# Row products that read PSUM, GpSimd low parts and later activation loads in a one-core transformer block

## The chip, the core and the metric

The kernel runs on one core of a Trainium2 chip. The core has a matrix engine (TensorE, PE in the profile), a vector engine (VectorE, DVE), a scalar engine (ScalarE, ACT), GpSimd (POOL) and a sync engine (SyncE, SP) that here only issues DMAs. ACT and POOL issue DMAs as well. Each engine works through its own queue in order. The engines share the on-chip memory SBUF; matmuls write into eight banks of a second memory, PSUM, each 128 partitions by 512 float32.

The metric is the time of one execution on the device in microseconds. A kernel's time is the median of several executions, and beside it stands one execution recorded by the profiler.

## What is computed

The reference is one block of a streaming encoder over 512 frames and 16 meta tokens of width 2048: two attention branches, gated and merged, and then a product-key expert layer with 16,384 experts of which each token uses 128. The expert layer matters here:

```python
def block(xb):
    q = (xb @ w_q).reshape(PEER_BLOCK, PEER_HEADS, 2, PEER_HALF)
    s = jnp.einsum('thcd,hcnd->thcn', q, sub_keys).astype(jnp.float32)
    s1, i1 = lax.top_k(s[:, :, 0], PEER_TOPK)
    s2, i2 = lax.top_k(s[:, :, 1], PEER_TOPK)
...
    h = jnp.einsum('tkd,td->tk', u[idx], xb)
    act = (g * jax.nn.gelu(h.astype(jnp.float32), approximate=False)).astype(xb.dtype)
    return jnp.einsum('tk,tkd->td', act, v[idx])
```

Then the result is added to the residual, and a final RMSNorm over the 2048 features ends the kernel.

## The kernel before

**Splitting of operands.** All large products are done as three passes on a high and a low part of each operand (`mm3`, L259). `wtile` (L233) loads a raw weight tile of 128x1024 (SP, L244), makes the high part on ACT (L246) and the low part by a subtraction (L247), on DVE unless an engine is named. It notes the last ACT instruction in `more["last"]`, and the last low part in `more["lo"]` if it was not on POOL.

**The stages in time.** Attention and gates run to about 1310 us. Then comes the score stage: 16 blocks `hc`, each with two weight tiles `wq` and a query result `ps`, which ACT and DVE split into `pqh` and `pql` (L265, L266), and 12 small matmuls of the block before (`scores`, L1138), which DVE ranks with `top16` (L940). Most low parts of this stage are made on POOL.

After it the expert layer has two phases. In the first, 128 blocks `e` compute h for 128 experts each, for the first 324 tokens (ND): `u_products` (L1115) has two halves `hf`, each one weight tile and 24 matmuls; ACT takes the Gelu of the result (L1407) and sends it to DRAM. In the second, 32 steps `i` of eight weight tiles multiply the gated activations with v and add into `acc` (L1541). The activations of a group of four blocks come back from DRAM with two loads, `hin` (L1363) and `gin` (L1355); they are gated (`gated`, L1369) and split (`group_split`, L1442).

**The remaining 188 tokens** go another way, by gathered rows. `send` (L1063) has POOL issue an indirect DMA that brings one row of u or v for each of 128 partitions; `row_step` (L1087) has DVE multiply it. A u row is multiplied with the tokens' activations and summed over the row (L1095); the activations of the first 128 tokens (part 0) are `xg`, 128x2048, in SBUF. `PACE` (L1051) ties the number of rows done to the block: 20 before the first block, 38 by block 14, 108 by block 60. By block 16 that is some 41 rows, all of part 0.

**Routing.** `route` (L967) finds the experts of the first 324 tokens in small DVE steps between the blocks (`beside`, L1391); `gates_of` (L1263) turns them into a dense gate.

**Order.** The framework places each instruction of a queue when its inputs are ready by its own model, in the order of the program among those that are ready; a dependency without synchronisation (`NOSYNC`) only keeps one instruction behind another in that order. So a load can be placed long before the line that asks for it is reached, and then its queue waits at it until its buffer is free. `spread_rows` (L957), called at block 64, issues eight small loads on SP.

**PSUM.** One pool of eight banks serves all stages (`ps_tile`, L225).

**The end.** Each finished chunk of `acc` is squared on ACT into `fsq` (one buffer) and added to `ssf` on DVE (`fin_add`, L1453). `fin_out` (L1460) sums `ssf` over partitions with a matmul by ones, forms the reciprocal root (`rstd`, L298), scales 16 chunks on DVE (L1465) and stores them from SP (L1467).

## Time and profile before

| | us |
|---|---|
| median of 3 runs | 3480.44 |
| lowest and highest | 3478.97, 3483.09 |
| the profiled execution | 3478.44 |
| its span | 3476.4 |

The span runs from the first to the last instruction of the program. A row of a view names a line of the kernel, an engine, an operation and the tiles as out<-in. Behind a bar, or in square brackets, stands the idle time of the engine before the instruction and what ended it: "<-DVE wl L247" means that DVE's instruction on line 247 that wrote `wl` released it. "SPq" and "DMA" rows are issues of DMAs. The granted clock is TensorE's, as a share of full speed.

### The profile page before, as it was taken

Reading aid. Unit: us, or ns where it says so; the run is one execution under the profiler, and the core shown is the slowest. Engines: PE = TensorE matmul, PEld = TensorE weight load, DVE = VectorE, ACT = ScalarE, POOL = GpSimd, SP = SyncE. Lnnn points to the kernel's source line nnn. Section 1 sums busy time; section 2 is a strip of 40 time slices with the busy share of each in tenths; the row PEclk is TensorE's granted clock in tenths of the full one; section 3 lists DMA queues with packets and bytes.
Section 4 is the critical chain, followed back from the end, with each engine's and each line's share of the span. In section 5 each row is a group of like instructions: output and inputs, shape, how many; then the busy total and the mean of one; then the engine's idle time right before and its main releaser. Section 6 shows DMA issues by size and latency. Waiting matters only on the chain.

```text
span 3476.4 us, 53485 instructions
## 1 busy us (share of the span) xinstructions
PE 3419.8 (98%) x21140; PEld 3183.4 (92%) x21140; DVE 2589.1 (74%) x3584; ACT 1428.7 (41%) x2303; POOL 805.5 (23%) x575
## 2 busy tenths in 40 slices
PE   9999999999999999989999999999999999999997
PEld 8988888888888887879999999999999999999997
DVE  5533334435754557999999988887789998999997
ACT  4233333334543223223476776774333333333333
POOL 1000000000011114433233333333322322323230
PEclk9999999999999999999999999999999999999999
DMA  5332222232144345669999999999999999999993
GB/s 172 101 101 98 97 97 97 89 105 74 49 146 143 136 139 182 239 222 366 356 396 402 405 412 410 412 409 398 405 381 397 377 405 390 403 375 396 399 390 128
DMA packets 228873, 929.91 MB, mean 267 GB/s; under 512 B 28246, under 2 KB 53966, under 8 KB 179538
## 3 DMA queue, kind: packets, MB, share of 16 engines
q1 hardware_dynamic: 135234, 467.95, 36.6%
q0 software_dynamic: 61632, 420.03, 30.2%
q10 hardware_dynamic: 31755, 38.52, 3.1%
q8 instruction: 165, 2.70, 0.3%
q14 instruction: 87, 0.70, 0.1%
HBM read 864.77 MB, written 63.73 MB: 267 GB/s over the span
## 4 chain that ended last, share of the span: by engine, by line
PE 72%; DVE 17%; DMA 5%; issue 4%; ACT 1%; SPq 0%; POOL 0%; DVEq 0%; ACTq 0%; POOLq 0%
PE ps L260 23%; PE ps L262 22%; PE ps L261 22%; DVE row L1095 3%; DVE wl L247 3%; DMA wr<-vb 2%; DMA wr<-ut 2%; DVE xg L1103 1%; DVE hgl L247 1%; PE ps L1288 1%; DVE wk L944 1%; DMA wr<-front 1%; DVE acc L1103 1%; ACT wh L246 0%; DVE acc L1541 0%
## 5 line engine op out<-in xcount | busy, mean ns | idle before, releaser
L246 ACT ACTIVATE wh<-wr 128x1024 fp32r<-128x1024 f32 (+1 forms) x654 | 688.4, 1054 | 1428.5 <-PE ps L262 926.9
L247 DVE TENSOR_TENSOR wl<-wr,wh 128x1024 fp32r<-128x1024 f32 (+1 forms) x627 | 793.2, 1273 | 393.2 <-ACT wh L246 382.3
L260 PE MATMUL ps<-vah,wl 128*128 128x324 f32 x2048 | 639.0, 312 | 4.6 <-DVE acc L1541 2.3
L262 PE MATMUL ps<-vah,wh 128*128 128x324 f32 x2048 | 639.1, 312 | 0.0
L261 PE MATMUL ps<-val,wh 128*128 128x324 f32 x2048 | 638.6, 312 | 0.0
L260 PE MATMUL ps<-hgh,wl 128*128 128x324 f32 (+1 forms) x1488 | 494.1, 332 | 22.5 <-DVE wl L247 14.4
L262 PE MATMUL ps<-hgh,wh 128*128 128x324 f32 (+1 forms) x1488 | 488.7, 328 | 0.0
L261 PE MATMUL ps<-hgl,wh 128*128 128x324 f32 (+1 forms) x1488 | 488.2, 328 | 0.0
L260 PE MATMUL ps<-xh,wl 128*128 128x512 f32 (+1 forms) x1376 | 468.1, 340 | 1.2 <-ACT xh L367 1.1
L261 PE MATMUL ps<-xl,wh 128*128 128x512 f32 (+1 forms) x1376 | 464.9, 338 | 0.7 <-DVE xl L368 0.7
L262 PE MATMUL ps<-xh,wh 128*128 128x512 f32 (+1 forms) x1376 | 464.9, 338 | 0.0
L260 PEld LDWEIGHTS ps<-vah,wl 128*128 128x128 f32 x2048 | 387.1, 189 | 7.0 <-DVE acc L1541 3.4
L261 PEld LDWEIGHTS ps<-val,wh 128*128 128x128 f32 x2048 | 386.8, 189 | 0.0
L262 PEld LDWEIGHTS ps<-vah,wh 128*128 128x128 f32 x2048 | 386.6, 189 | 0.0
L260 PEld LDWEIGHTS ps<-hgh,wl 128*128 128x128 f32 x1488 | 283.1, 190 | 36.8 <-DVE wl L247 16.2
L1082 POOL DMA_INDIRECT row<-v,eo x128 | 196.2, 1533 | 504.5 <-DVE xg L1103 401.2
L1095 DVE SCALAR_TENSOR_TENSOR row<-row,xg 128x2048 f32<-128x2048 f32 x128 | 306.1, 2392 | 2.2 <-DMA row<-u,eo 2.2
L1103 DVE SCALAR_TENSOR_TENSOR xg<-row,act,xg 128x2048 f32<-128x2048 f32 x127 | 297.7, 2344 | 3.9 <-DMA row<-v,eo 3.9
L262 PEld LDWEIGHTS ps<-hgh,wh 128*128 128x128 f32 x1488 | 282.9, 190 | 12.2 <-issue 0.2
L261 PEld LDWEIGHTS ps<-hgl,wh 128*128 128x128 f32 x1488 | 283.2, 190 | 11.1
L260 PEld LDWEIGHTS ps<-xh,wl 128*128 128x128 f32 x1376 | 258.7, 188 | 30.1 <-ACT xh L367 3.0
L261 PEld LDWEIGHTS ps<-xl,wh 128*128 128x128 f32 x1376 | 259.2, 188 | 29.0 <-DVE xl L368 1.6
(525 smaller groups left out, 6132.2 us busy)
## 6 DMA issues: line engine op xcount, KB each, us to landing
wr<-ut SPq DMA_DIRECT2D x256, 512.0 KB
wr<-vb SPq DMA_DIRECT2D x256, 512.0 KB
wr<-front SPq DMA_DIRECT2D x238, 512.0 KB
g_d<-gb POOLq DMA_DIRECT2D x42, 512.0 KB
gin<-g_d SPq DMA_DIRECT2D x32, 672.0 KB
h_d<-hb ACTq DMA_DIRECT2D x128, 162.0 KB
hin<-h_d SPq DMA_DIRECT2D x32, 648.0 KB
gates<-gt ACTq DMA_DIRECT2D x32, 256.0 KB
```

The lines of the kernel that those rows point to most:

```text
L246: more["last"] = S.activation(hi[:, s], r, AF.Copy)
L247: sub = (eng or V).tensor_sub(lo[:, s], r, hi[:, s].bitcast(F32))
L260: T.matmul(ps, wl, xh, start=start, stop=False)
L261: T.matmul(ps, wh, xl, start=False, stop=False)
L262: T.matmul(ps, wh, xh, start=False, stop=stop)
L944: V.match_replace(wk, vals[:, :8], src, -3.0e38)
L1082: G.indirect_dma_start(out=row, out_offset=None, in_=a[src], in_offset=bass.IndirectOffsetOnAxis(ap=eos[part][:, k:k + 1], axis=0))
L1095: ins = V.scalar_tensor_tensor(row, row, 1.0, xs[part], ALU.mult, ALU.mult, accum_out=w)
L1103: ins = V.scalar_tensor_tensor(y, row, w, y, ALU.mult, ALU.add)
L1288: T.matmul(bank[:, o:o + P], ohs[q % 4][:, 1, :, t], wos[:, q % 4, c, :, t], start=c == 1, stop=c == 0)
```

## The change

Four things change.

1. After the merge of the attention branches the pool of eight PSUM banks is closed and one of four opened; the other four hold `xps`, a copy of `xg` that ACT makes in four pieces in score blocks 1 to 4. The products of u rows of part 0 read `xps`, not `xg`, until block 16 (`LOWS`). There the four banks are given back and a pool of eight is opened again.
2. In the first 16 blocks the low part of the second half's weight tile is made on POOL.
3. In the second phase the loads of a group's activations are no longer asked for right after the split of the group before. For steps 1 to 3 they are asked for at tile 2, 1 and 1 of the step that also gates them (at tile 3, `QM`), and from step 3 on at tile 5 for two groups ahead; each load is kept behind the high part of that tile's weights in the planned order.
4. The end is rewritten. `fsq` has two buffers. The last finished chunk isn't added to `ssf`: `fin_last` sums `ssf` and its square by two matmuls into one bank. `fin_end` forms the reciprocal root with one DVE instruction less, its last one writing PSUM. Chunks 11 to 15 are multiplied by their gain on ACT as they finish and by the root on POOL, and are stored from ACT's queue; DVE scales and SP stores the other 11.

```diff
+GIN = 2, 1, 1
...
+    def bank_pool(bufs):
+        banks8.close()
+        psum["p"] = banks8.enter_context(tc.tile_pool(name="psum", bufs=bufs, space=PSUM, reuse_waits="tile"))
...
     merge.close()
+    bank_pool(4)
+    in_banks = ExitStack()
+    xps = in_banks.enter_context(tc.tile_pool(name="rows_x", bufs=1, space=PSUM, reuse_waits="tile")).tile([P, D], F32, name="xps")
...
-            ins = V.scalar_tensor_tensor(row, row, 1.0, xs[part], ALU.mult, ALU.mult, accum_out=w)
+            assert gs["xps"] is None or part == 0
+            ins = V.scalar_tensor_tensor(row, row, 1.0, xs[part] if gs["xps"] is None else xps, ALU.mult, ALU.mult, accum_out=w)
...
+    LOWS = 16
+
     def u_products(e, beside=lambda hf: None):
         ps = ps_tile()
         for hf in range(2):
-            wh, wl = wtile(a["ut"][2 * e + hf])
+            wh, wl = wtile(a["ut"][2 * e + hf], G if e < LOWS and hf else V)
...
+            if 0 < hc < 5:
+                q = slice((hc - 1) * 512, hc * 512)
+                S.activation(xps[:, q], xg[:, q], AF.Copy)
...
-    def group_in(g):
+    def group_in(g, mark=None):
         if g not in held:
             ht = hin_tile()
-            SP.dma_start(ht, h_d[g])
-            held[g] = [ht, group_g(g)]
+            lh = SP.dma_start(ht, h_d[g])
+            gt, lg = group_g(g)
+            held[g] = [ht, gt]
+            if mark is not None:
+                for ld in (lh, lg):
+                    tc.add_manual_dep(ld.ins, mark.ins.name, NOSYNC, reason="not before its buffer is free")
...
+        if e == LOWS:
+            assert not banks
+            gs["xps"] = None
+            in_banks.close()
+            bank_pool(8)
...
-        sq = ssf if first else vp.tile([P, SEQ], F32, name="fsq", bufs=1)
+        sq = ssf if first else vp.tile([P, SEQ], F32, name="fsq", bufs=2)
...
+    BESIDE = 11
+    final = {}
+
+    def fin_last(c):
+        ps = final["ps"] = ps_tile()
+        T.matmul(ps[:, :ND], ones, ssf[:, :ND], start=True, stop=False)
+        sq = vp.tile([P, SEQ], F32, name="fsq", bufs=2)
+        S.activation(sq[:, :ND], acc[:, c, :ND], AF.Square)
+        T.matmul(ps[:, :ND], ones, sq[:, :ND], start=False, stop=True)
+
+    def fin_end():
+        sc = vp.tile([P, D], F32, name="sc", tag="row", bufs=1).rearrange("p (k t) -> p k t", t=SEQ)
+        v, r0, t = (sc[:, k, :ND] for k in range(3))
+        ps, rp_ = final["ps"][:, :ND], ps_tile()[:, :ND]
+        S.activation(t, ps, AF.Ln, scale=1.0 / D, bias=C("eps"))
+        V.tensor_scalar(v, ps, 1.0 / D, EPS, ALU.mult, ALU.add)
+        S.activation(r0, t, AF.Exp, scale=-0.5)
+        V.tensor_mul(v, v, r0)
+        V.scalar_tensor_tensor(v, v, -0.5, r0, ALU.mult, ALU.mult)
+        V.scalar_tensor_tensor(rp_, v, 1.5, r0, ALU.add, ALU.mult)
+        S.activation(rf[:, :ND], rp_, AF.Copy)
+        for c0, n in ((11, 2), (13, 2), (15, 1)):
+            for c in range(c0, c0 + n):
+                G.tensor_mul(acc[:, c, :ND], acc[:, c, :ND], rf[:, :ND])
+            S.dma_start(a["out"][c0:c0 + n, :, :ND].rearrange("k p t -> p k t"), acc[:, c0:c0 + n, :ND])
+        for c0, n in ((0, 1), (1, 2), (3, 3), (6, 3), (9, 2)):
+            for c in range(c0, c0 + n):
+                V.scalar_tensor_tensor(acc[:, c, :ND], acc[:, c, :ND], gain("fin")[:, c:c + 1],
+                                       rp_, ALU.mult, ALU.mult)
+            SP.dma_start(a["out"][c0:c0 + n, :, :ND].rearrange("k p t -> p k t"), acc[:, c0:c0 + n, :ND])
...
                 group_split(i + 1)
-                if i + 2 < NG:
-                    group_in(i + 2)
+                if 3 <= i < NG - 2:
+                    group_in(i + 2, more["last"])
+            if 1 <= i <= 3 and qi == GIN[i - 1]:
+                group_in(i + 1, more["last"])
...
                 if i >= NG - 1 and not stays:
-                    fin_add(c, 0, ND, not done)
+                    if len(done) == KC - 1:
+                        assert c < BESIDE
+                        fin_last(c)
+                    else:
+                        fin_add(c, 0, ND, not done)
+                    if c >= BESIDE:
+                        S.activation(acc[:, c, :ND], acc[:, c, :ND], AF.Copy, scale=gain("fin")[:, c:c + 1])
                     done.append(c)
...
-    fin_out(0, ND)
+    fin_end()
     fin.close()
     rt.close()
+    banks8.close()
```

More of the change, by code (lines that the diff above doesn't have):

```diff
@@ L221, in body @@
     wp = top.enter_context(tc.tile_pool(name="weights", bufs=3, side="left"))
-    pp = top.enter_context(tc.tile_pool(name="psum", bufs=8, space=PSUM))
+    banks8 = ExitStack()
+    psum = {"p": banks8.enter_context(tc.tile_pool(name="psum", bufs=8, space=PSUM))}
     dp = top.enter_context(tc.tile_pool(name="dram", bufs=1, space=DRAM))
     def ps_tile(name="ps"):
-        return pp.tile([P, 512], F32, name=name, tag="ps")
+        return psum["p"].tile([P, 512], F32, name=name, tag="ps")
+    def bank_pool(bufs):
+        banks8.close()
+        psum["p"] = banks8.enter_context(tc.tile_pool(name="psum", bufs=bufs, space=PSUM, reuse_waits="tile"))
     more = {"n": 0, "pool": None, "tails": None}
@@ L1058, in body @@
     rcols = [rcol] + [rcolb[:, j:j + 1] for j in range(len(cuts))]
-    gs = {"sent": 0, "done": 0, "pool": None, "gated": False, "six": None, "third": False, "x": 1, "rows": None, "vi": None, "early": None}
+    gs = {"sent": 0, "done": 0, "pool": None, "gated": False, "six": None, "third": False, "x": 1, "rows": None, "vi": None, "early": None, "xps": xps}
     rows = {}
@@ L1354, in group_g @@
         gt = gt.rearrange("p (b j t) -> p b j t", j=GRP, t=TH)
-        SP.dma_start(gt, g_d[g])
-        return gt
+        return gt, SP.dma_start(gt, g_d[g])
     held = {}
-    def group_in(g):
+    def group_in(g, mark=None):
         if g not in held:
             ht = hin_tile()
-            SP.dma_start(ht, h_d[g])
-            held[g] = [ht, group_g(g)]
+            lh = SP.dma_start(ht, h_d[g])
[4 more added lines that the diff above has]
+                    tc.add_manual_dep(ld.ins, mark.ins.name, NOSYNC, reason="not before its buffer is free")
     def follows(ins, what):
```

## The prediction

> **What bounds the kernel now.** I read the totals of the page first, then the busy time by stretches, then what TensorE (PE) waited for, then single instructions where it waited longest.
>
> ```profile
> span 3476.4 us, 53485 instructions
> ## 1 busy us (share of the span) xinstructions
> PE 3419.8 (98%) x21140; PEld 3183.4 (92%) x21140; DVE 2589.1 (74%) x3584; ACT 1428.7 (41%) x2303; POOL 805.5 (23%) x575
> ```
>
> PE is busy for 3419.8 of 3476.4 us, and the change takes no expert matmul away. What can be won is therefore PE's idle time, 56.6 us, and time in which PE runs at a lower granted clock. So I ask where these lie. The columns of the next view are PE, PEld, DVE, ACT, POOL, then clock, DMA share and GB/s.
>
> ```profile
> 1400.00:1527.00 127.00, 116.44 (x544) 94.82 (x542) 122.94 (x399) 29.19 (x38) 57.37 (x36) 0.97 0.63 226
> 1527.00:1597.00 70.00, 61.58 (x361) 59.16 (x361) 67.96 (x209) 22.30 (x27) 20.84 (x14) 0.90 0.84 323
> 1597.00:1667.00 70.00, 70.00 (x470) 69.80 (x471) 70.00 (x122) 24.55 (x30) 22.50 (x14) 1.00 0.96 370
> ```
>
> The first row is the second half of the score stage, the second the first expert blocks (0 to about 5), the third blocks 6 to 15. In the first two PE idles for 10.6 and 8.4 us while VectorE (DVE) is busy for 122.94 of 127 and 67.96 of 70 us: here DVE is the limit. In the third both are full and PE loses nothing. The waits between 1400 and 1600 us say the same, and add to 19.0 us:
>
> ```profile
> PE ps L260 <- DVE wl L247: 9.4, 4, 4.1
> PE ps L260 <- POOL wl L247: 5.3, 1, 5.3
> PE ps L260 <- DVE hgl L247: 3.1, 1, 3.1
> PE ps L260 <- DVE pql L266: 1.2, 2, 0.9
> ```
>
> The lower clock costs PE at most (1-0.97) x 127 + (1-0.90) x 70 = 10.8 us more. The longest wait shows why DVE is late:
>
> ```profile
> 1479.82 4.66 POOL L247 TENSOR_TENSOR wl<-wr,wh 128x1024 fp32r<-128x1024 f32 x2
> 1480.61 0.67 DVE L266 TENSOR_TENSOR pql<-ps,pqh 128x512 fp32r<-128x512 f32 x1
> 1481.20 5.43 DVE L1095 SCALAR_TENSOR_TENSOR row<-row,xg 128x2048 f32<-128x2048 f32 x1
> 1482.22 0.80 PE L260 MATMUL ps<-hgh,wl 128*128 128x512 f32 x1 [5.31 <-POOL wl L247]
> ```
>
> While GpSimd (POOL) makes two low parts, DVE's `pql`, which has one operand in PSUM, takes its usual 0.67 us. The row product after it, whose two operands are both in SBUF, gets nowhere until POOL is done at 1484.48 and takes 5.43 us.
>
> **Part 1: the row products read PSUM.** `xps` replaces `xg` as second operand of the part-0 rows up to block 16. What such a product costs with POOL at work and without:
>
> ```profile
> L1095 DVE SCALAR_TENSOR_TENSOR row<-row,xg 128x2048 f32<-128x2048 f32 x17 | 53.2, 3132 | 2.2 <-DMA row<-u,eo 2.2
> L1095 DVE SCALAR_TENSOR_TENSOR row<-row,xg 128x2048 f32<-128x2048 f32 x23 | 52.4, 2276 | 0.0
> L862 DVE TENSOR_TENSOR g<-g,ps 128x512 f32<-128x512 f32 x7 | 4.8, 687 | 17.3 <-PE ps L262 17.3
> L266 DVE TENSOR_TENSOR mgl<-g,mgh 128x512 fp32r<-128x512 f32 x4 | 2.7, 677 | 0.0
> ```
>
> The first row holds the 17 products of 1400 to 1527 us, beside POOL's low parts; the second the 23 of 1537 to 1667 us, where POOL makes none. The first 17 pay 53.2 - 17 x 2.276 = **14.5 us** for the overlap, and `pql` above says that an operand in PSUM ends that. No row shows this instruction with a PSUM operand. The other two rows bound what it costs by itself: with PSUM 687 ns, without 677, for 512 columns. I take 0 (40 ns a row over 41 rows would be 1.6 us; a gain beyond the overlap is excluded, since `g<-g,ps` is no faster). The four copies that fill `xps` are ACT work, and ACT is busy for 29.19 of 127 us: nothing, and some 2 us if ACT were full.
>
> **Part 2: POOL takes the odd half's low part of 16 blocks.** The low parts of 1527 to 1667 us on DVE, by stretch, then the three rows that price one elsewhere: POOL's own and its gathers between 1300 and 1714 us, and DVE's low part between 1100 and 1300 us, where POOL works on `hsq` beside it.
>
> ```profile
> 1527.00:1597.00 70.00, 17.01 (x14) 0.00 (x0) 0.90 0.84 323
> 1597.00:1667.00 70.00, 25.32 (x21) 0.00 (x0) 1.00 0.96 370
> L247 POOL TENSOR_TENSOR wl<-wr,wh 128x1024 fp32r<-128x1024 f32 x27 | 66.9, 2488 | 47.7 <-ACT wh L246 47.4
> L1082 POOL DMA_INDIRECT row<-u,eo x55 | 73.7, 1339 | 203.1 <-DVE row L1095 59.5 <-DVE tv L945 42.9 <-DVE wk L944 32.4
> L247 DVE TENSOR_TENSOR wl<-wr,wh 128x1024 fp32r<-128x1024 f32 x37 | 63.1, 1706 | 33.4 <-ACT wh L246 33.4
> ```
>
> One low part is 17.01/14 = 1.21 us, so DVE loses 16 x 1.21 = 19.4 us of work, 7 x 1.21 = **8.5 us** of it before 1597. Against that POOL's 2.49 us per block now meet DVE's remaining low part and the routing's two-operand instructions. A collision costs between 0 and 2.49 us. The nearest row has 1.706 - 1.21 = 0.5 us a low part; I take that once per block, 7 x 0.5 = **3.5 us** back.
>
> The rule of the Trainium skill (SBUF — State Buffer, Who interferes with whom) speaks against this part: the port that VectorE and GpSimd share is an exclusive lock held for a whole instruction, so each of the 16 low parts may hold a two-operand VectorE instruction for all its length. By the rule at its worst the sum would get 16 x 2.49 = 40 us back against 19.4 saved. The trace agrees with the lock (the row product's 5.43 us), but its mean of 0.5 us a low part says that few meet head on, and the sum goes by that.
>
> **What that is worth to PE.** DVE has 14.5 + 8.5 - 3.5 = **19.5 us** less to do by 1597 us, and was full until then, so its deadlines come 19.5 us earlier. PE could take up to 19.0 + 10.8 = 29.8, so DVE stays the limit and PE gains 19.5. The nine lows after 1597 (10.9 us of DVE) gain nothing: PE has 70.00 of 70 there already.
>
> The next wait is not DVE's doing and stays. In the rows below SP's queue, held by the small loads of `spread_rows`, brings a weight tile late to ACT, and PE idles 3.73 us:
>
> ```profile
> 1692.78 0.34 SPq L960 DMA_DIRECT2D eob<-eob_d  x1
> 1702.92 1.06 ACT L246 ACTIVATE wh<-wr 128x1024 fp32r<-128x1024 f32 x1 [7.34 <-DMA wr<-ut]
> 1708.51 0.42 PE L260 MATMUL ps<-hgh,wl 128*128 128x324 f32 x1 [3.73 <-DVE wl L247]
> ```
>
> The stalls' second price is the clock: 0.90 in the stretch where the longest single wait is 4.1 us. The Trainium skill (TensorE: Matmul & The Clock Gate, Part 1) has the clock halved after an idle window of about 3.4 us. By that page only the stalls of 5.3 and 4.1 us would cost clock and PE's limit would be near 19 + 2 x 1.7 = 22 us; the rows' 10.8 us say that shorter stalls cost it too, and the limit above goes by the rows.
>
> **Part 3: four banks instead of eight.** What decides is how long a bank is held. Here the ACT half of a score block's result is read at once, the DVE half 11 us later:
>
> ```profile
> 1443.81 0.60 ACT L265 ACTIVATE pqh<-ps 128x512 fp32r<-128x512 f32 x1 [4.49 <-PE ps L262]
> 1455.05 0.68 DVE L266 TENSOR_TENSOR pql<-ps,pqh 128x512 fp32r<-128x512 f32 x1
> 1456.34 0.60 ACT L265 ACTIVATE pqh<-ps 128x512 fp32r<-128x512 f32 x1 [4.49 <-DVE ef L1015]
> ```
>
> A block is 1456.34 - 1443.81 = 12.5 us and takes two banks, so with four the first is wanted again 12.5 us after it is full, and it is free after 11.9. With 14.5 us less backlog the cover is wide: 0. If it is gone, PE waits as for `pql` now (1.2 us). Changing pools twice may hold one block until its bank is read, 0 to 1 us each; I take 0.
>
> **Part 4: activation loads.** SP waits at these loads for buffers, with weight loads behind them; whether PE cares, the waits from 2490 to 3460 us show:
>
> ```profile
> SPq L1363 <- DVE val L266: 65.5, 19, 6.7
> SPq L1355 <- DVE hin L1375: 59.6, 28, 4.2
> PE ps L260 <- DVE acc L1541: 2.3, 3, 0.9
> PE ps L260 <- DVE wl L247: 1.8, 4, 0.6
> ```
>
> PE's waits there are 4.1 us and none names a load: at most 4.1 gained. A load that is sent one or two weight tiles before its product, as in steps 1 to 3, could hold DVE; three times 2 us would be the loss. I take 0.
>
> **Part 5: the end.** After the last matmul all is on the path:
>
> ```profile
> 3459.51 0.50 DVE L1458 TENSOR_TENSOR ssf<-ssf,fsq 128x324 f32<-128x324 f32 x1 [0.60 <-ACT fsq L1456]
> 3460.06 1.45 PE L302 MATMUL ps<-ssf,cst 128*128 128x324 f32 x2 [2.31 <-DVE ssf L1458]
> 3461.55 0.53 ACT L310 ACTIVATE sc<-ps,cst 128x324 f32<-128x324 f32 x1 [2.07 <-PE ps L302]
> 3464.03 0.50 DVE L316 TENSOR_TENSOR rf<-sc 128x324 f32<-128x324 f32 x1
> 3464.57 7.55 DVE L1465 SCALAR_TENSOR_TENSOR acc<-acc,gn,rf 128x324 f32<-128x324 f32 x16
> L640 POOL TENSOR_TENSOR qrr<-qrr,cos_t 128x512 f32<-128x512 f32 x4 | 5.1, 1278 | 70.9 <-PE ps L638 70.9
> L640 POOL TENSOR_TENSOR krs<-krs,cos_t 128x264 f32<-128x264 f32 x2 | 1.5, 750 | 34.7 <-PE ps L638 34.7
> ```
>
> The last `ssf` add goes (0.55 with its hand-over); the sum over the first 15 chunks overlaps the last chunk's square: 0.6. From Ln to `rf` one instruction less: 3.0 us becomes 2.6. DVE scales 11 chunks instead of 16: 5 x 7.55/16 = 2.4. POOL's five, between 0.75 and 1.28 us each, about 0.88 at 324 columns, take 4.4 us beside DVE's 5.2. The last store is two chunks, not one: 166 KB more, 0.4 us at the 370 GB/s of the third stretch. The sum is 0.6 + 0.4 + 2.4 - 0.4, **3 us**.
>
> **The sum.** 19.5 + 3 = 22.5 us. The profiled execution took 3478.4 us for its span of 3476.4; that leaves 3455.9. The median of the three runs, 3480.4, is 2 us above it: **3458 us**.
>
> **Rivals.**
> - All stalls to 1600 us go (DVE's order changes so that low parts come ahead of rows): 29.8 + 3, so 3448; with the 1708 stall, 3.7 and its clock loss of about 1.7, 3442. For it: deadlines, not sums, make stalls, and rows can wait. Against it: DVE's 67.96 of 70. Chance 0.18.
> - POOL's low part comes late behind a gather. In POOL's queue a gather waits for a row buffer that DVE frees (idle 203.1 us before 55 gathers). Two waits like the 5.3 us one cost 10.6: 3468. Chance 0.17.
> - The same mechanism, worse, in the 16 blocks: each wait is 5.3 plus some 1.7 us of clock, 7 us. From the fourth on (22.5/7 = 3.2) the change is slower; six make +42 - 22.5, so 3500. For it: such a wait happened once in 27 low parts with three weight buffers. Against it: DVE has less backlog, so buffers come free sooner. Chance 0.06.
> - The change doesn't do what it says: the product from PSUM is held as before, or four banks stall PE for what is gained. Then only the end is left, 3477. Against it: `pql` at 0.67 us. Chance 0.06.
>
> **How the numbers follow.** The forecast has the remaining 0.53, by itself 3449 to 3467 (collisions from 0 to 1.8 us a low part: +3.5 to -9). The range, 3443 to 3472, adds the first two rivals. A measurement of this kernel can tell about 0.2%, 7 us, from no change. Faster: 0.53 + 0.18 + 0.17 = 0.88; same 0.06; slower 0.06.
>
> **What would show it.** Right: products of `xps` at 2.3 us beside POOL's low parts, no wait of PE on POOL near 1480, PE's waits between 1400 and 1600 below 10 us, clock there above 0.95, the 1708 stall still there, some 16 us from the last expert matmul to the end instead of 18.6 (3476.4 less 3460.06 - 2.31). Wrong: products above 3 us, waits on POOL `wl` in blocks 0 to 15, waits on `ps` readers, DVE idle before gated products in the second phase.

## The result, and the profile after

The changed kernel takes 3499.68 us (median of 6 runs, 3496.61 to 3504.29) against 3482.23 us for the kernel before in the same job (6 runs, 3478.97 to 3485.47). The ratio is 1.0052, with a 95% interval of 1.0039 to 1.0065: slower by half a per cent, where 3458 us was forecast. The profiled execution took 3504.29 us, the longest of its six; it is 25.9 us above the profiled one of the kernel before, where the medians are 17.45 us apart. The traces below therefore show a larger loss than the medians. In the kernel after, a line has a number 6 to 56 higher than in the kernel before: the low parts are L253 (before L247), the row products L1105 (L1095), the add into `acc` in the second phase L1597 (L1541).

The totals of the page after:

```profile
span 3502.5 us, 53549 instructions
PE 3427.2 (98%) x21142; PEld 3189.6 (91%) x21142; DVE 2588.4 (74%) x3561; ACT 1432.9 (41%) x2313; POOL 838.8 (24%) x596
```

The span is 26.1 us longer, PE's busy time 7.4 us, so PE's idle time grew from 56.6 to 75.3 us. The same three stretches as before (the columns are PE, PEld, DVE, ACT, POOL, clock, DMA share, GB/s):

```profile
1400.00:1527.00 127.00, 124.78 (x596) 102.51 (x595) 119.67 (x423) 31.10 (x41) 61.82 (x38) 1.00 0.66 242
1527.00:1597.00 70.00, 63.35 (x408) 62.88 (x408) 66.98 (x174) 25.70 (x31) 39.02 (x23) 0.95 0.89 345
1597.00:1667.00 70.00, 55.38 (x338) 53.79 (x337) 69.35 (x123) 21.17 (x25) 25.64 (x16) 0.93 0.79 277
```

The first stretch did what was forecast: PE is busy for 124.78 us instead of 116.44, at a clock of 1.00 instead of 0.97. The third did not. It had no PE idle time before; now PE is busy for 55.38 of 70 us while DVE is as full as it was (69.35). PE's waits between 1400 and 1600 us, then those between 1600 and 1720 us, then those of the second phase between 2490 and 3460 us (total, times, longest; three answers of the view of waits):

```profile
PE ps L266 <- DVE wl L253: 5.2, 2, 3.5
PE ps L266 <- DVE hgl L253: 3.2, 1, 3.2
PE ps L266 <- POOL wl L253: 0.5, 1, 0.5
```

```profile
PE ps L266 <- DVE wl L253: 11.6, 4, 4.3
PE ps L266 <- DVE hgl L253: 3.0, 2, 1.5
```

```profile
PE ps L266 <- DVE acc L1597: 12.1, 10, 3.9
PE ps L266 <- DVE wl L253: 3.9, 4, 1.5
```

Up to 1600 us the waits fell from 19.0 to 8.9 us. In the second answer stood one wait of 3.7 us before; now there are 14.6 us. In the third stood 2.3 and 1.8 us; waits on `acc` alone are now 12.1. All are waits on DVE, almost none on POOL.

Where the time went, from the start of each piece of work in the two traces (us from the start of the span):

| | before | after | difference |
|---|---|---|---|
| first score product | 1314.4 | 1318.7 | +4.3 |
| expert block 0 | 1538.0 | 1532.7 | -5.3 |
| expert block 6 | 1592.5 | 1583.5 | -9.0 |
| expert block 16 | 1665.1 | 1674.8 | +9.7 |
| expert block 24 | 1729.0 | 1733.3 | +4.3 |
| expert block 48 | 1911.6 | 1924.6 | +13.0 |
| second phase | 2515.7 | 2525.9 | +10.2 |
| last product of the second phase | 3457.4 | 3485.5 | +28.0 |
| end | 3476.4 | 3502.5 | +26.1 |

So there are two losses, 18.7 us in blocks 6 to 15 and 17.8 us in the second phase, and a smaller one of 4.3 us ahead of the score stage. They outweigh a gain of 9.0 us up to block 6.

### The profile page after: what moved, and what is told of

It is laid out like the page before. It is cut to its first block, busy times and chain, and to the rows that moved or that the text cites. A ratio compares the mean times of both kernels' runs of the same rounds, so it can differ in the third digit from the quotient of the medians.

```text
span 3502.5 us, 53549 instructions
## 1 busy us (share of the span) xinstructions
PE 3427.2 (98%) x21142; PEld 3189.6 (91%) x21142; DVE 2588.4 (74%) x3561; ACT 1432.9 (41%) x2313; POOL 838.8 (24%) x596
## 4 chain that ended last, share of the span: by engine, by line
PE 65%; DVE 18%; issue 8%; DMA 7%; POOL 2%; ACT 1%; SPq 0%; DVEq 0%; ACTq 0%; POOLq 0%
PE ps L266 20%; PE ps L267 20%; PE ps L268 20%; DMA wr<-vb 4%; DVE wl L253 3%; DVE row L1105 3%; DVE xg L1113 2%; POOL row L1091 1%; DVE xgb L1113 1%; PE ps L1303 1%; DVE hgl L253 1%; DMA g_d<-gb 1%; DVE acc L1113 1%; ACT wh L252 1%; DMA wr<-front 1%
## 5 line engine op out<-in xcount | busy, mean ns | idle before, releaser
L253 DVE TENSOR_TENSOR wl<-wr,wh 128x1024 fp32r<-128x1024 f32 (+1 forms) x617 | 785.7, 1282 | 415.2 <-ACT wh L252 409.7
L266 PE MATMUL ps<-vah,wl 128*128 128x324 f32 x2048 | 641.7, 313 | 16.5 <-DVE acc L1597 12.1
L268 PEld LDWEIGHTS ps<-xh,wh 128*128 128x128 f32 x1376 | 258.5, 188 | 27.3
```

The source lines that it names most:

```text
L253: sub = (eng or V).tensor_sub(lo[:, s], r, hi[:, s].bitcast(F32))
L266: T.matmul(ps, wl, xh, start=start, stop=False)
L268: T.matmul(ps, wh, xh, start=False, stop=stop)
```

## The experiments

The theory after these views: (A) POOL's low parts hold DVE in blocks 6 to 15; (B) the four banks cost PE at their beginning; (C) the activation loads, now sent in pairs, make weight tiles late in the second phase. The main rival to A was that the gain of the rows is lost in another way, by the banks; the main rival to C that the second phase only suffers from work that blocks 6 to 15 left behind. All ratios are against the kernel before in the same job, with 95% intervals.

| run | kernel | ratio | interval |
|---|---|---|---|
| after | the whole change | 1.0052 | 1.0039 to 1.0065 |
| e1 | the change, all low parts on DVE | 1.0038 | 1.0022 to 1.0053 |
| e2 | the change, loads as before | 1.0022 | 1.0012 to 1.0032 |
| e3 | the change without both | 0.9986 | 0.9973 to 0.9999 |
| e4 | before, and the 16 low parts | 1.0070 | 1.0053 to 1.0086 |
| e5 | before, and the four banks, empty | 1.0013 | 1.0002 to 1.0025 |
| e6 | e3, rows from PSUM and banks up to block 1 | 0.9979 | 0.9967 to 0.9991 |
| e7 | six low parts, banks up to block 6, loads as before | 0.9963 | 0.9952 to 0.9975 |
| e8 | before, and the new end | 0.9992 | 0.9981 to 1.0003 |
| e9 | e7, the banks opened five score blocks later | 0.9951 | 0.9937 to 0.9965 |
| e10 | e7, loads tied but apart | 0.9981 | 0.9971 to 0.9992 |
| e11 | e3, low parts of blocks 6 to 15 on POOL | 1.0002 | 0.9993 to 1.0011 |
| e12 | before, and the tied loads | 1.0035 | 1.0022 to 1.0048 |
| e13 | before, and loads tied but apart | 1.0012 | 1.0002 to 1.0023 |

### e1, e2 and e3: the change without its low parts, without its loads, without both

```diff
# e1 and e3
-            wh, wl = wtile(a["ut"][2 * e + hf], G if e < LOWS and hf else V)
+            wh, wl = wtile(a["ut"][2 * e + hf], V)
# e2 and e3
-                if 3 <= i < NG - 2:
-                    group_in(i + 2, more["last"])
-            if 1 <= i <= 3 and qi == GIN[i - 1]:
-                group_in(i + 1, more["last"])
+                if i + 2 < NG:
+                    group_in(i + 2)
```

> The changed kernel with all low parts of the blocks on DVE again; xps, four banks, the loads and the end stay. Theory A (POOL's low parts hold DVE): in the changed kernel's trace PE is 18.7 us later by block 16 than it would be with its lead at block 6 kept, and DVE's two-operand instructions there take 2 to 3 us beside POOL's low parts. Without them the 18.7 us come back: ratio to before about 1.000 (17.4 - 18.7 = -1 us; 3481), PE's waits in blocks 6 to 15 below 4 us instead of 15. Rival B (four banks or the pools' exchange make the blocks late): waits in blocks 6 to 15 stay, ratio stays near 1.005. In both cases some 12 us are still lost in the second phase.

> The changed kernel with the activation loads asked for where before asks for them. Theory C (hin and gin now leave back to back, 1.3 MB in one burst, and the next weight tiles land late): the second phase's loss of some 12 to 15 us goes, ACT's longest wait for a weight tile falls from 9 to below 7 us, SP's waits at the two loads return (about 120 us); ratio about 1.001 (17.4 - 14 = +3 us; 3485). Rival D (the second phase is late because of the order of DVE's row products, which the rest of the change moved): waits on acc of some 12 us stay, ratio near 1.005.

> Both undone at once: what is left is xps with its four banks, and the new end. Theories A and C together: 17.4 - 18.7 - 14 = -15 us, ratio about 0.9955 (3467), which is the row products' 14.5 us less the exchange of pools plus the end's 2 to 3 us. Rivals B and D: 1.003 to 1.005.

Without POOL's low parts blocks 6 to 15 take 74.1 us instead of 91.3 (before: 72.6), which is A. The ratio of e1, 1.0038, missed the 1.000 that A gave all the same: the executions of this kernel lie between 3482 and 3498 us, the profiled one was the shortest of them, and in it, too, the second phase is 9 us longer than before. The interval of e1 overlaps that of the change, so by the times A rests on e2 and e3, which differ in the low parts alone (1.0022 and 0.9986, blocks 6 to 15 at 91.0 and 74.0 us), and on e4 below. With the loads as before the second phase keeps its length: in e2 the kernel is 13.1 us late at its start and 10.3 us late at its end, against 10.2 and 28.0 in the change. That is C, and the rival to C falls, since e2 has the same backlog from blocks 6 to 15. Its ratio, 1.0022, is a little above the 1.001 expected. Between e1 and e3 the loads are worth 0.5%, between the change and e2 0.3%.

The ratio of e3 was missed: 0.9955 was expected, 0.9986 came. What is left there, rows from PSUM, banks and end, gains 5 us and not 15. In its profile block 6 starts 3.3 us later than before, with waits of 2.5 us near 1318, of 3.3 us on `pql` near 1389 and of 4.5 us on ACT's `hb` at 1560, none of which the kernel before has. Blocks 0 to 5 take 61.4 us instead of 54.5, though DVE's rows cost it less. That led to e5 and e6.

### e4: the low parts alone

```diff
-            wh, wl = wtile(a["ut"][2 * e + hf])
+            wh, wl = wtile(a["ut"][2 * e + hf], G if e < 16 and hf else V)
```

> The kernel before with POOL making the odd half's low part of blocks 0 to 15 and nothing else: row products read xg in SBUF. Theory A: each of 16 low parts holds DVE for about 2 us (row products now too, up to 2.4 us each) against 1.21 us saved, so 16 x 0.8 = 13 us and more are lost: ratio 1.004 to 1.008 (3495 to 3510), row products of 4 to 5 us appear after 1540 us. Rival (the collisions matter only with the new bank or load order): 0.996 to 1.001, because DVE saves 19 us of work.

The time came as expected, its detail did not. Blocks 6 to 15 take 93.1 us instead of 72.6, but few row products are held (2470 ns in the mean, where 2276 is one by itself); it is mostly the routing that is, as the second of these two groups of DVE between 1575 and 1687 us of e4 shows, a cast that takes 0.3 us by itself:

```profile
L1095 DVE SCALAR_TENSOR_TENSOR row<-row,xg 128x2048 f32<-128x2048 f32 x17 | 41.9, 2470 | 0.0
...
L975 DVE CAST i1f<-lists 128x128 f16<-128x128 uint32 x3 | 5.4, 1807 | 0.0
```

In the changed kernel, where the rows read PSUM, the same can be followed most clearly. One low part on POOL, and what DVE does meanwhile (start and duration in us):

```profile
1631.38 2.42 POOL L253 TENSOR_TENSOR hgl<-wr,hgh 128x1024 fp32r<-128x1024 f32 x1
```

```profile
1627.77 2.27 DVE L1105 SCALAR_TENSOR_TENSOR row<-row,xps 128x2048 f32<-128x2048 f32 x1
...
1630.72 0.16 DVE L992 COPY step<-i1f 128x4 f16<-128x4 f16 x1
1630.79 3.07 DVE L993 TENSOR_TENSOR step<-i1f 128x60 f16<-128x60 f16 x1
1633.78 0.44 DVE L951 MAX8 tv<-cand 128x8 f32<-128x112 f32 x2
...
1635.95 1.21 DVE L253 TENSOR_TENSOR wl<-wr,wh 128x1024 fp32r<-128x1024 f32 x1
```

A tensor operation on 60 columns takes 3.07 us; it ends at 1633.86, just after POOL's low part (1633.80). Its record starts 0.6 us before that of the low part, so the trace shows that the two end together and not how they met. DVE's own low part, 1.21 us, for which PE waits, comes after it. The groups of DVE between 1573 and 1677 us of the changed kernel in which instructions were held like this (count, then busy time in us and mean in ns over held and free ones):

```profile
L253 DVE TENSOR_TENSOR wl<-wr,wh 128x1024 fp32r<-128x1024 f32 x7 | 12.6, 1794 | 0.5 <-ACT wh L252 0.5
L253 DVE TENSOR_TENSOR hgl<-wr,hgh 128x1024 fp32r<-128x1024 f32 x6 | 9.2, 1532 | 0.0
...
L1019 DVE TENSOR_TENSOR oh<-pb,tables 128x1024 f16<-128x1024 f16 x2 | 3.7, 1836 | 0.0
L1012 DVE TENSOR_TENSOR pb<-pb,tmp 128x64 f16<-128x64 f16 x2 | 3.5, 1750 | 0.1
L993 DVE TENSOR_TENSOR step<-i1f 128x60 f16<-128x60 f16 x3 | 3.4, 1141 | 0.0
L992 DVE COPY step<-i1f 128x4 f16<-128x4 f16 x3 | 3.3, 1109 | 0.0
L1038 DVE TENSOR_TENSOR gw_all<-gw_all,gsum 128x128 f32<-128x128 f32 x2 | 2.7, 1334 | 0.0
```

The same instructions in e7 between 1575 and 1662 us, where POOL makes no low parts in these blocks:

```profile
L253 DVE TENSOR_TENSOR wl<-wr,wh 128x1024 fp32r<-128x1024 f32 x13 | 15.8, 1217 | 0.3 <-ACT wh L252 0.3
L253 DVE TENSOR_TENSOR hgl<-wr,hgh 128x1024 fp32r<-128x1024 f32 x10 | 12.2, 1221 | 0.9 <-ACT hgh L252 0.9
...
L1019 DVE TENSOR_TENSOR oh<-pb,tables 128x1024 f16<-128x1024 f16 x1 | 0.7, 693 | 0.0
L1012 DVE TENSOR_TENSOR pb<-pb,tmp 128x64 f16<-128x64 f16 x2 | 0.6, 304 | 0.0
...
L993 DVE TENSOR_TENSOR step<-i1f 128x60 f16<-128x60 f16 x2 | 0.4, 184 | 0.0
L992 DVE COPY step<-i1f 128x4 f16<-128x4 f16 x2 | 0.3, 164 | 0.0
L1038 DVE TENSOR_TENSOR gw_all<-gw_all,gsum 128x128 f32<-128x128 f32 x1 | 0.3, 279 | 0.0
```

The difference of the means, times the counts, is 4.0 + 1.9 + 2.3 + 2.9 + 2.9 + 2.8 + 2.1 = 18.9 us; an `oh<-oh,i1f` of 512 columns adds 1.2. So ten low parts hold DVE for 20.1 us, 2.0 us each, while the same ten save it 10 x 1.22 = 12.2 us. DVE has no slack against PE there, and the blocks grow by 18.7 us, more than the net 8 us of DVE; 121 routing instructions fall into them instead of 96.

### e5 and e6: the four banks alone, and the rows in the score stage alone

```diff
# e5: the kernel before, with four banks from the score stage to block 16, and no xps
+    bank_pool(4)
+        if e == 16:
+            bank_pool(8)
# e6: e3 with
-    LOWS = 16
+    LOWS = 1
```

In e6 the constant sets only the block from which rows read `xg` and eight banks are back; all low parts are on DVE.

> The kernel before with the pool of four banks between the merge and block 16; the other four banks lie idle, rows read xg in SBUF, no copies. Theory E (four banks by themselves stall PE): the same waits as in the run with both parts undone appear, 2.5 us at the exchange near 1317 us, 3.3 us on pql near 1387 and 2 to 5 us on the Gelu's read of block 0 near 1559, 8 to 10 us with the clock's 1 to 2 more: ratio 1.002 to 1.004 (3487 to 3494). Rival (these waits come from the copies into xps or from DVE's new order, banks are free in time): ratio 0.999 to 1.001.

> Low parts on DVE, loads as before, new end; xps and four banks only until block 1, then eight banks and rows from xg. Rows meet POOL's low parts only in the score stage, so DVE's 14.5 us stay saved. Theory E: the wait on block 0's Gelu goes, and PE's waits in blocks 1 to 6 fall: 4 to 8 us better than with the banks held to block 16, ratio about 0.997 (3470). Rival (PE's waits in the first blocks come from DVE's order alone): as with the banks held, 0.9985 (3475).

The banks alone cost 0.13%, 4.5 us, which lies between what the theory (1.002 to 1.004) and its rival (0.999 to 1.001) gave; the interval reaches into both. Two new waits show where it is lost. The view of waits between 1300 and 1400 us has them word for word the same in the change, e5 and e7 but for line numbers; in the change:

```profile
PE ps L266 <- DVE pql L272: 3.3, 1, 3.3
PE ps L893 <- ACT xg L894: 2.5, 1, 2.5
```

The second is the exchange of the pools itself: a transposition for the last chunk waits for a bank that ACT still reads. The first comes in score block 4, which takes two banks more than the others for transposed factors; with four in all, PE waits until DVE has made `pql`, and DVE is first busy for 5.7 us with four copies for those factors. The wait on `hb` at 1560 us did not come in e5, so it isn't the banks' alone, and e6, which has eight banks from block 1, is without it. The ratio of e6, 0.9979, lies between the values of its two theories (0.997 and 0.9985), and its interval takes in both. From e6 and e8 (0.9992) the rows from PSUM with their banks are worth some 0.13%, with intervals that overlap.

### e7 and e11: low parts in blocks 0 to 5 only, and in blocks 6 to 15 only

```diff
# e7: the change with
-    LOWS = 16
+    LOWS = 6
# and the loads as in e2; e11: LOWS = 16, loads as in e2, and
-            wh, wl = wtile(a["ut"][2 * e + hf], G if e < LOWS and hf else V)
+            wh, wl = wtile(a["ut"][2 * e + hf], G if 6 <= e < LOWS and hf else V)
```

> Low parts on POOL, xps and four banks in blocks 0 to 5 only; loads as before, new end. Theory A with the trace of the changed kernel (each low on POOL holds DVE for 2 us; the cost shows from block 6 on): block 6 starts near 1584 us as there (-9 against before) and blocks 6 to 16 take 73 to 75 us instead of 91; with the end's -2 ratio 0.996 to 0.998 (3466 to 3473). Rival (the lost time comes whenever POOL has had lows in the blocks, since routing is brought forward and then held): ratio 1.000 to 1.002.

> e7's kernel with the low parts of POOL in blocks 6 to 15 instead of 0 to 5 (row products from PSUM up to block 16, loads as before, new end). Theory (the place decides: from block 6 on DVE runs routing work on SBUF operands and has 0 us of slack against PE, and each low part of 2.4 us on POOL holds it): blocks 6 to 15 take 85 to 95 us instead of 75, ratio 1.000 to 1.003. Rival (the number decides: the first few low parts are free wherever they are, later ones pay): the first five blocks lose under 3 us, blocks 6 to 15 take under 82 us, ratio 0.997 to 0.999.

e7 beats both kernels: 3467.05 us (9 runs), 0.9963. Blocks 0 to 5 take 49.5 us instead of 61.4 in e3, where rows read PSUM there too, 58.5 in e6, and 54.5 before; the six low parts hold DVE for 3.2 us in all, 0.5 us each. During the first four, DVE is at work on rows from PSUM and on the top-16 search (MAX8, FIND_INDEX8), which aren't held: of the search, a FIND_INDEX8 beside POOL takes 0.27 us as it does without.

e11 came out between its two theories. Its ratio is the one of the theory of the place, but blocks 6 to 15 take 74.8 us, not 85 to 95 (74.0 in e3, which has no low parts on POOL); in its profile it falls behind e3 later, by 5 us in blocks 24 to 47 and by 6 us in the second phase. Some of DVE's groups of e11 between 1586 and 1673 us show that ten low parts hold it there, too:

```profile
L253 DVE TENSOR_TENSOR hgl<-wr,hgh 128x1024 fp32r<-128x1024 f32 x5 | 7.3, 1469 | 0.0
...
L1021 DVE TENSOR_TENSOR oh<-oh,i1f 128x1024 f16<-128x1024 f16 x2 | 3.6, 1788 | 0.0
L992 DVE COPY step<-i1f 128x4 f16<-128x4 f16 x3 | 2.7, 892 | 0.0
...
L1038 DVE TENSOR_TENSOR gw_all<-gw_all,gsum 128x128 f32<-128x128 f32 x1 | 2.4, 2449 | 0.0
```

Summed as above over all held instructions it is 12.0 us, 1.2 us each, which takes back just what ten low parts save (12.2). So the place decides whether a low part pays (0.5 us each in blocks 0 to 5 against 1.2 and 2.0 in 6 to 15, for 1.22 saved). That it not only fails to pay but costs 18.7 us takes both halves: e7 and e11 have one half each and take 75 us for blocks 6 to 15, the change, e2 and e4 have both and take 91 to 93. With the first six on POOL as well, 34 routing instructions of DVE fall into blocks 0 to 5 instead of 69 in e11, and 121 instead of 83 into blocks 6 to 15 (e4: 35 and 145). That this shift of the routing is the reason is read from the counts and not shown: longer blocks also have room for more of them, and no run changed the order of the routing.

### e8 and e9: the new end alone, and the banks opened later

```diff
# e8: the kernel before with fsq bufs=2, fin_last and fin_end of the change
# e9: e7 with
-    bank_pool(4)
...
-            if 0 < hc < 5:
-                q = slice((hc - 1) * 512, hc * 512)
-                S.activation(xps[:, q], xg[:, q], AF.Copy)
+            if hc == 5:
+                bank_pool(4)
+                xps = in_banks.enter_context(tc.tile_pool(name="rows_x", bufs=1, space=PSUM, reuse_waits="tile")).tile([P, D], F32, name="xps")
+            if 5 <= hc < 7:
+                for h in range(2):
+                    q = slice((2 * hc - 10 + h) * 512, (2 * hc - 9 + h) * 512)
+                    S.activation(xps[:, q], xg[:, q], AF.Copy)
+                if hc == 6:
+                    gs["xps"] = xps
```

> The kernel before with the new end alone. The sum on record: 3 us; the trace of the changed kernel had 17.0 us from the last expert matmul to the end instead of 19.0: -2 us, ratio 0.9993 (3478), clear of no change only if the interval is narrow. Rival (the second buffer for the squares or the gains on ACT slow the last steps): 1.000 to 1.001.

> e7 (first six lows, loads as before) with one thing moved: the four-bank pool and xps are opened in score block 5 instead of ahead of the score stage, so the exchange and the second bank pair of score block 4 meet eight banks; the row products of score blocks 5 and 6 (about three) read SBUF as before. Theory (the stay in four banks costs at its beginning, by the exchange and by the two extra banks of block 4): PE's waits of 2.5 us near 1317 and 3.3 us near 1387 go, three row products pay up to 0.9 us each; the milestones at e0 come 3 to 6 us earlier than in e7; ratio 0.9945 to 0.9955. Rival (an exchange costs wherever it is made): a wait of 2 to 4 us turns up near 1390 instead, ratio 0.996 to 0.997 as in e7.

e8 has the size expected, and its interval takes in no change. In e9 both waits of the four banks are gone; between 1300 and 1400 us there is only this one left:

```profile
PE ps L266 <- POOL wl L253: 1.6, 1, 1.6
```

The score stage starts 0.4 us later than before and not 5.4, block 0 is 9.9 us earlier and not 2.3. This is the theory, and e9 has the lowest ratio of all (3467.97 us against 3482.06, 0.9951). Its interval overlaps that of e7, which ran in another job, so which of the two is faster isn't settled by the times.

### e10, e12 and e13: the loads by themselves, in pairs and apart

```diff
# e12: the kernel before with the loads of the change
# e10 (on e7) and e13 (on the kernel before): the same, but instead of the pair
# hin alone at tile 5 of a step and gin at tile 7
-                    group_in(i + 2, more["last"])
+                    hin_in(i + 2, more["last"])
+            if 3 <= i < NG - 2 and qi == 7:
+                held[i + 2].append(gin_in(i + 2, more["last"]))
```

> e7 with the activation loads tied to weight tiles as in the change, but hin is sent at the fifth and gin at the seventh tile of a step instead of back to back (steps 1 to 3 as in the change). Theory (the burst of two loads delays the weight tile behind them): with the loads some 8 us apart the second phase keeps its length, Vend minus V start within 3 us of e7's, no PE wait above 2.5 us behind a load; ratio 0.995 to 0.997. Rival (the tie itself costs, because a load that waits for a product holds SP's queue or DVE): the second phase loses 9 to 18 us as in e1 and in the changed kernel, ratio 0.999 to 1.002.

> The kernel before with the change's activation loads alone (hin and gin tied to weight tiles, sent back to back). Theory (the burst of two loads delays the weight tile behind it): the second phase from the first to the last gated product grows by 6 to 18 us from 941.7 us, PE waits of 1.5 to 4 us appear behind pairs of loads; ratio 1.002 to 1.005. Rival (the loss needs the other parts, which only shift the phase of the loads): second phase within 3 us, ratio 0.999 to 1.001.

> As e12, but gin is sent at the seventh weight tile of a step and hin at the fifth. Theory (burst): second phase within 3 us of before's 941.7 us, ratio 0.999 to 1.001, clearly below e12. Rival (the tie itself costs, burst or not): as e12, 1.002 to 1.005; from e10, which gave 0.0018 more than e7, some 6 us.

e12 alone costs 0.35% and shows the loss on a kernel that has nothing else of the change: its second phase takes 958.0 us instead of 941.7. How it comes about can be followed in the changed kernel. SP's queue sends the pair at 2883.8 and 2884.7 us, weight loads behind it; ACT has been idle for 9.08 us when the weight tile behind them comes; DVE, which has run out of work, makes its low part at 2903.7; and the add into `acc`, for whose bank PE waits, is at 2918.1 (SP, ACT and DVE of one timeline view each; in brackets the idle time before and what ended it):

```profile
2860.47 23.29 SPq L250 DMA_DIRECT2D wr<-vb  x7
2883.82 0.87 SPq L1377 DMA_DIRECT2D hin<-h_d  x1
2884.74 0.73 SPq L1370 DMA_DIRECT2D gin<-g_d  x1
2889.14 27.17 SPq L250 DMA_DIRECT2D wr<-vb  x8
```

```profile
2902.63 1.06 ACT L252 ACTIVATE wh<-wr 128x1024 fp32r<-128x1024 f32 x1 [9.08 <-DMA wr<-vb]
```

```profile
2903.72 1.23 DVE L253 TENSOR_TENSOR wl<-wr,wh 128x1024 fp32r<-128x1024 f32 x1 [6.32 <-ACT wh L252]
...
2914.73 1.22 DVE L253 TENSOR_TENSOR wl<-wr,wh 128x1024 fp32r<-128x1024 f32 x1
2915.86 2.35 DVE L1113 SCALAR_TENSOR_TENSOR acc<-row,actb,acc 128x2048 f32<-128x2048 f32 x1
2918.13 0.49 DVE L1597 TENSOR_TENSOR acc<-acc,ps 128x324 f32<-128x324 f32 x1
```

The 6.32 us in which DVE stands idle are gone for good: four row sums of 2.35 us are due in the same stretch, DVE does them between its low parts, and PE waits 3.86 us at 2918.7. The two loads are 648 and 672 KB, more than two weight tiles of 512 KB, and the DMA share between 2890 and 2900 us is 1.02: the transfers are at their limit, so the tile behind the pair has to wait for both. Before, they left 4 to 21 us apart between 2600 and 2700 us (`gin` at 2603.17, `hin` at 2616.77, for instance).

With the pair apart most of the waits on `acc` go, and not all of the loss: both e10 (0.995 to 0.997 expected) and e13 (0.999 to 1.001) came out above their theory. The waits of PE between 2490 and 3460 us, first of e12, then of e13:

```profile
PE ps L261 <- DVE acc L1547: 14.1, 10, 3.8
PE ps L261 <- DVE wl L248: 0.8, 2, 0.6
```

```profile
PE ps L261 <- DVE wl L248: 8.4, 9, 1.8
PE ps L261 <- DVE acc L1560: 2.0, 2, 1.1
```

Waits on `acc` fall from 14.1 to 2.0 us, and the ratio from 1.0035 to 1.0012; up to step 28 of the second phase e13 loses 3.3 us and e12 16.3. But waits on low parts rise to 8.4 us, most near the end, so that over the whole phase e13 loses 10.9 us and e12 16.3; the profiled execution of e13 is the longest of its twelve, 7 us above their median. e10 is 0.18% above e7, which ran in another job, and its second phase is 3.5 us longer. So, by the medians, the burst is the larger part. The rest, about a third (0.0012 of 0.0035, with an interval from 0.0002 to 0.0023), is the price of the tie by itself or of its new place, which these runs don't settle; e11, whose loads are as before, loses 3.4 us from step 28 on as well.

## Why the prediction was wrong

**What bounds the kernel** was read rightly: DVE was the limit from 1400 to 1597 us, and relieving it there moved PE. The forecast had block 6 start 19.5 us earlier; it starts 9.0 us earlier. The step from DVE's sum to PE's gain was too simple by itself: in e3 the rows save DVE the same 14.5 us, and block 0 starts 3.6 us earlier but block 6 3.3 us later than before. By the counts 69 routing instructions of DVE fall into blocks 0 to 5 there instead of 43, so part of what DVE saved went to work that PE wasn't waiting for. No run shows how much.

**Part 1, the row products.** Right in mechanism and size, as time of DVE. In the changed kernel, between 1400 and 1527 us, beside POOL's low parts:

```profile
L1105 DVE SCALAR_TENSOR_TENSOR row<-row,xps 128x2048 f32<-128x2048 f32 x18 | 41.0, 2275 | 2.7 <-DMA row<-u,eo 2.7
```

A product takes 2275 ns where it took 3132, 14.6 us for 17, against 14.5 forecast; the PSUM operand costs nothing by itself. PE does not wait for POOL near 1480 any more.

**Part 2, POOL's low parts: the step that failed most.** The price of a collision was taken from low parts beside `hsq` between 1100 and 1300 us, 0.5 us, and was asked only of the seven up to 1597. POOL's operations there are shorter, too: 1.0 and 1.3 us in the mean, against 2.4 for a low part. For the six of blocks 0 to 5 that holds: 3.2 us in e7, and 4.4 us in the change, 0.5 to 0.7 each. For the other ten it is 2.0 us each. What stands beside them decides: there DVE runs routing on SBUF operands, and no row of the stretch 1100 to 1300 says what that pays. The forecast then called those nine or ten "gain nothing", as PE had 70.00 of 70 us; but DVE had 70.00 of 70 too, so whatever they took from DVE was PE's loss. It was 18.7 us. The rule of the Trainium skill (SBUF — State Buffer, Who interferes with whom) at its worst gave 40 us for 16, an estimate, and the mean of 0.5 gives 8; the change shows 4.4 + 20.1 = 24.5, about halfway, and e4 27. The same section of the Trainium skill names copies and casts among what can be held, not two-operand instructions alone, and says that a reduction isn't; the traces agree with both, a COPY of four columns at 1109 ns in the mean instead of 164, and `ef`, a reduction, at 0.68 us throughout. The prediction had only two-operand instructions in view.

**Part 3, four banks.** Taken at 0, measured at 0.13% by e5. The step compared one tile's hold, 11.9 us, with one block, 12.5. It did not ask which block takes more than two banks (block 4) nor who still reads one when the pools change; the bound of "0 to 1 us" for an exchange was too low against 2.5 us.

**Part 4, the loads.** Taken at 0, measured at 0.35% by e12. The step looked at what the waits of before could yield, 4.1 us, and at loads too close to their product, and not at two loads that now leave one after the other: SP's waits at them, 65.5 and 59.6 us before, had kept them apart. That was a stall which did useful work.

**Part 5, the end.** 3 us forecast, 1.9 by the marker that was given (16.7 us from the last expert matmul to the end, instead of 18.6). Its timeline (DVE, then SP) in the changed kernel:

```profile
3490.02 0.50 DVE L1511 SCALAR_TENSOR_TENSOR ps<-sc 128x324 f32<-128x324 f32 x1
3491.03 5.17 DVE L1519 SCALAR_TENSOR_TENSOR acc<-acc,gn,ps 128x324 f32<-128x324 f32 x11 [0.51 <-ACT rf L1512]
```

```profile
3491.61 5.00 SPq L1521 DMA_DIRECT2D out<-acc  x5
```

The 11 scalings take 5.17 us, as forecast, 2.4 us less than 16. From the last matmul to the first scaling it is 5.2 us instead of 6.8, 1.6 gained where 1.0 was forecast. The mis-sized term is the last store: from the last scaling (3496.20) to the end it is 6.3 us and not 4.3 as before, 2.0 lost where 0.4 was put. Whether that is its size or the stores that ACT sends beside it, no run tells.

**Of the signs that were named**, the products at 2.3 us, no wait on POOL near 1480, waits below 10 us up to 1600 (8.9) and the clock (0.98 over these 200 us) came as they should; all of them look at the part that worked. Of the signs of being wrong one came, waits on readers of banks (3.3 us on `pql`, 2.5 on ACT's copy into `xg`); none named the routing instructions of DVE beside POOL. **The stall at 1708** was to stay. In the change it is gone (blocks 16 to 23 take 5.4 us less), in e7 and e9, which reach it earlier, it is there with 3.1 and 3.2 us. It depends on when PE comes by, and was no fixed cost.

**The rivals.** The third, 3500 us, has the time that came, by luck and not by its mechanism: PE waits for POOL's low parts not once in blocks 0 to 15 (0.5 us ahead of them), where the rival had 5.3 us each time. It asked whether POOL would be late; POOL was in time, and made DVE late. No rival had the loads. The bound of 3449 us for the forecast by itself doesn't follow from its terms: no collisions at all give 3.5 us more, 3454.5.

**The sum, corrected**, between the two traces: -9.0 up to block 6, +18.7 in blocks 6 to 15, +0.5 from there to the second phase, +17.8 in it, -1.9 at the end: +26.1. The steps in the +0.5 are larger than their sum (-5.4 up to block 24, +8.7 up to 48, -2.8 after that); blocks 24 to 47 took 182 to 191 us in the various runs. There is a pattern: the five runs with 196 to 199 routing instructions of DVE in these blocks (the change, e2, e4, e6, e11) take 188 to 191 us, the ten with 167 to 189 take 182 to 185. Four of the five have POOL's low parts in blocks 6 to 15; what puts the routing there stays open.

## What to carry to other kernels

Work moved to GpSimd is paid by what VectorE runs at that moment: take the price of a collision from the instructions of that stretch, per operation, and where VectorE is full, count it as time of the whole. The good half of such a change is then found by place: six low parts beside PSUM rows and searches made their blocks 9 us shorter (e7 against e6), ten beside routing gained nothing (e11) or, with the first six, lost 18.7. A stall that spreads transfers is not slack: before it goes, look at what will leave back to back; and when buffers are halved, list the block that takes the most of them and the readers at the moment of the exchange.

## What the runs showed of the hardware

- Beside a GpSimd operation of two SBUF operands (2.4 us here), VectorE's tensor operations on two SBUF operands, copies, casts and tensor-scalar operations can be held until it is done, however small they are (60 columns: 3.07 us instead of 0.18; a tensor-scalar operation of 64 columns in e4: 3.13 instead of 0.19). With one operand in PSUM (row products, 2275 ns), in MAX8 and FIND_INDEX8 and in reductions (`ef`, 0.68 us) no instruction was held. Which of a mix is hit is a matter of order: 0.5 us a low part in one stretch, 2.0 in the next.
- Short stalls can cost clock here, and their length alone doesn't decide it. Between 1597 and 1667 us the mean granted clock is 0.93, some 4.9 us of 70, with six waits. In stretches of 4 us the clock falls at two of them: to 0.62 (1602 to 1606) behind one of 2.4 us, and to 0.78, 0.50 and 0.86 (1654 to 1666) during and behind one of 4.3 us. Behind the other four, one of 3.1 us among them, it stays at 1.00. The Trainium skill (TensorE: Matmul & The Clock Gate, Part 1) has the clock halved after an idle window of about 3.4 us; by that the wait of 4.3 us alone would have cost one window at half speed, some 1.7 us, an estimate from that page. The trace has some 3.4 us there, 0.9 of it while PE still waits, and some 1.7 behind the wait of 2.4 us.
- Two loads of 1.3 MB in all, sent one behind the other at a DMA share of 1.0, left the engine behind them without its 512 KB weight tile for 9 us; the same loads sent two tiles apart cost PE 12 us less in waits on `acc` over the phase (14.1 against 2.0), and 7.6 us more in waits on low parts (0.8 against 8.4).
